# Windowed attention of a two-layer encoder: its loops taken apart into seven streams, TensorE's order written out

## The chip, the cores and the metric

One core of a Trainium2 chip runs the whole program. The metric is device time in microseconds (us), the median of repeated executions. TensorE is PE in the rows (its weight loads PEld), VectorE is DVE, ScalarE is ACT, GpSimd is POOL, SyncE is SP.

## The reference, cut to what matters

An encoder of two layers over 256 tokens of 1024 channels. Layer 0 mixes tokens by a recurrence (RWKV-7), layer 1 by attention; each layer is followed by a mixture of 32 experts (MoE), of which a token uses two. Each sub-layer is normalised, shifted, scaled and gated by six vectors ("modulations") computed from a conditioning vector. The change touches layer 1's attention alone:

```python
qkv = jnp.einsum('bsd,de->bse', h, w_qkv)            # 1024 -> 9216: 3 groups x (q,k,v) x 8 heads x 128
for gi, (window, dil) in enumerate(ATTN_GROUPS):     # (128,1), (512,4), (2048,16)
    o, lse = _dilated_group(q, k, v, slopes[gi], window, dil)   # softmax(q k / sqrt(128) - slope*|distance|) v
alpha = jax.nn.softmax(jnp.stack(lses), axis=0)      # the three groups weighed by their denominators
merged = jnp.sum(alpha[..., None] * o, axis=0)
return jnp.einsum('bsd,de->bse', merged, w_o)
```

## The kernel before, in words

Matmuls of the attention run on pairs of 16-bit numbers: `split` (L461) makes of a float32 tile a high half on ScalarE and the rest, a low half, on VectorE (or on GpSimd, L467, for the second half of two weight tiles in three), and `triple` (L1712) issues three matmuls: high by high, low by high, high by low.

**Projections.** `heads` (L1722) goes through four pairs of heads (hp), three groups (g) and q, k, v (j): 36 projections. Each takes one 1 MB weight tile off the ring `wring`, splits it in two halves (`weights`, L1703; two buffers of each kind, so that half n is split when half n-2 has been multiplied), and issues 8 steps of 6 matmuls of 256 columns into one of three PSUM banks (`pp`). The result is split again (`qh`, `ql`).

**Scores and values.** For a pair and a group, `scores` (L1788) multiplies q by k, adds the distance term and takes the maximum on VectorE (L1800, L1803), and takes exponentials with their sums on ScalarE (L1809). `merge` (L1812) makes of maxima and sums of the three groups the weights `wg`, in some fifteen VectorE operations on 4 elements a partition. `values` (L1831), for each of two heads, multiplies the exponentials by `wg` on VectorE (L1837), transposes them on TensorE (`eT`), splits them, multiplies them by v (`av`) and splits the result into `mh`, `ml`. The tiles of exponentials E exist once, so a pair's scores wait for the values of the pair before. Group 0's scores follow the projections of group 1; those of groups 1 and 2 follow the projections of group 2 (loop at L1873).

**Modulations.** 32 parts, each a 512 KB row block of `w_ada` off a ring of two (`aring`), are multiplied and added into `acc` on VectorE (L374, L376): four parts behind each of the first eight groups (L1881). After eight parts `ada` (L428) sums `acc` over the partitions on TensorE. For vectors 2 and 5 (the gates `ga`) this is one float32 product for each half of the columns, and each is added on VectorE (L448) to a bias that a DMA on ScalarE's queue brings (L442, held behind what ScalarE was given before it). There is one PSUM bank (`ada`) for all of this.

**Output.** `out_pairs` (L1693) scales the four weight tiles of the output projection by the gate on GpSimd (L590), splits and multiplies them (`wo`). Three of the four run while the last pair's values wait.

**Order.** A scheduler places each engine's instructions by priority (the order of the program text) as its own cost estimates let them become ready; a matmul of the attention may so be placed before or after its neighbours in the text. In layer 0, `weave` (L277) is used: generators (streams) yield, an account adds up TensorE's estimated time, `RANK` chooses among the streams that are ready, `OFFSET` shifts the priority of what a stream issues, and TensorE's instructions are pinned to that order (L263). All weight tiles (layer 0, MoE 0, qkv, output, MoE 1) come in one order through one ring on SP's queue, and a load starts when a buffer is free. The attention frees buffers for MoE 1's weights as it ends. What follows the attention is MoE 1 (`moe`, L1369) in eight quarters of 12 tiles, and the final norm.

Of the kernel before, what the change touches and what calls it, by code (L numbers as in the profile page):

```python
# [19 lines left out]
D = 1024  # L20
S = 256
# [213 lines left out]
def trunk(ctx, tc, names, aps, out, stages=("rwkv", "moe0", "attn", "moe1"), dbg=None, ring=2):  # L235
# [189 lines left out]

    ada_acc, modulations_attn = [], []

    def ada(i, m, k, tag="ps"):  # L428
# [9 lines left out]
        if k < KD - 1:  # L438
            return
        if m in (2, 5):  # L440
            g = gates[i, m] = const.tile([128, D], F32, name=f"ga{m}", tag=f"ga{m}", bufs=1)
            bias = nc.scalar.dma_start(out=g, in_=ap["p_adab"][i:i + 1, m * D:(m + 1) * D].to_broadcast([128, D]))  # L442
            tc.keep_in_program_order(bias)
            for c in range(2):
                s = slice(c * 512, c * 512 + 512)
                ps = bank(name="ada", tag=tag)
                mm(ps, ONES, acc[:, s])
                V.tensor_tensor(out=g[:, s], in0=g[:, s], in1=ps, op=ALU.add)  # L448
        else:
            ps = bank(name="ada", tag=tag)  # L450
            for n in range(8):
                mm(ps[:, n:n + 1], acc[:, n * 128:(n + 1) * 128], ONES[:, 0:1])
            ada_due.append((i, m, ps))
# [1268 lines left out]
    def heads(outer, mh, ml, before, c4):  # L1722
# [42 lines left out]
        QK = XSC * XSC  # L1765
        scale = 128 ** -0.5

        def project(hp, g):
            out = []
            for j in range(3):  # L1770
                with tc.issue_after(heads.hi[5].ins) if hp + g == 0 and j == 1 else nullcontext():
                    w = heads.w if hp + g + j == 0 else weights(
                        outer, stream.take(("qkv", hp, g, j)).rearrange("p (k n) -> p k n", k=KD),
                        pool_half=j != 1 and hp + g > 0)
                ps = bank(name="qkv", tag="pp")
                t = [(held, pool)[j // 2].tile([128, 2, S], F16, name=f"q{n}{g}{j}", bufs=1) for n in "hl"]
                for k in range(KD):
                    hk = (hh[:, k], hl[:, k])
                    lhs, rhs = (w[k], hk) if j < 2 else (hk, w[k])
# [4 lines left out]
                split(*(v.rearrange("p a n -> p (a n)") for v in t), ps, (scale if j == 0 else 1.0) / WSC)  # L1784
                out.append(t)
            return out

        def scores(hp, g, qkv, E, st):  # L1788

            q, k, _ = qkv  # L1790
            w = KW[g]
            for a in range(2):
                ps = bank(name="sc", tag="sc")
                for t in range(NTT):
# [6 lines left out]
                                       in1=ps[:, 0:NTT * w].rearrange("p (t n) -> p t n", t=NTT),  # L1801
                                       op0=ALU.mult, op1=ALU.add)
                V.tensor_reduce(out=st[:, :, a, 0], in_=e, axis=AX.X, op=ALU.max)  # L1803
            neg = pool.tile([128, NTT, 2], F32, name="neg", bufs=2)
            V.tensor_scalar(out=neg, in0=st[:, :, :, 0], scalar1=-1.0 / QK, scalar2=None, op0=ALU.mult)
            for a in range(2):
# [24 lines left out]
        def values(hp, a, qkv, E, wg):  # L1831

            eh, el = (pool.tile([128, 8, 128], F16, name=n) for n in ("eh", "el"))
            for g in range(3):
                for t in range(NTT):
                    e = E[g][:, a, t * KW[g]:(t + 1) * KW[g]]
                    V.tensor_scalar(out=e, in0=e, scalar1=wg[:, t, g, a:a + 1], scalar2=None, op0=ALU.mult)  # L1837
            blocks = [E[0][:, a, t * 256 + kt * 128:t * 256 + kt * 128 + 128] for kt in range(2) for t in range(NTT)]
            blocks += [E[g][:, a, t * 128:(t + 1) * 128] for g in (1, 2) for t in range(NTT)]
            for n in range(2):  # L1840
                ps = bank(name="eT", tag="eT")
                for b in range(4):
                    tr(ps[:, b * 128:(b + 1) * 128], blocks[4 * n + b])
                split(*(v[:, 4 * n:4 * n + 4].rearrange("p b n -> p (b n)") for v in (eh, el)), ps, WSC)
            po = bank(name="av", tag="eT")
            vcol = slice(a * 128, a * 128 + 128)

            def av(o, v, c, start, stop):
                triple(o, [t[:, v[1], vcol] for t in qkv[v[0]][2]],
                       [t[:, c].rearrange("p b n -> p (b n)") for t in (eh, el)], start, stop)  # L1850

            for kt in range(2):
# [5 lines left out]
            split(*(v[:, 2 * hp + a].rearrange("p (l r) -> p r l", r=NTT) for v in (mh, ml)),  # L1858
                  po[:, 0:S].rearrange("p (r l) -> p r l", r=NTT), 1.0 / WSC)

        c4.enter_context(banks(pp=3, sc=2, eT=2, ada=1))
        apool1 = modulations_of_attention()
        if "moe1" in stages:
            ext.extend(middle(1, 3))
        attn_shares = iter(ADA_ATTN)
        for hp in range(4):
            if hp == 3:
                modulations_attn[0].done()
                apool1.release()
                if "moe1" in stages:  # L1870
                    ext.extend(middle(1, 0))
            qkv, E, st = [], [], []
            for g in range(4):  # L1873
                if g < 3:
                    qkv.append(project(hp, g))
                for n in range(max(0, g - 1), g):
                    E.append(pool.tile([128, 2, NTT * KW[n]], F32, name=f"E{n}", bufs=1))
                    st.append(pool.tile([128, NTT, 2, 2], F32, name=f"st{n}", bufs=2))
                    scores(hp, n, qkv[n], E[n], st[n])
                if g < 3 and hp < 3:  # L1880
                    for a in itertools.islice(attn_shares, ADA_PARTS[3 * hp + g]):  # L1881
                        ada(*a, "ada")
            if hp == 3:
                held.release()
                if "moe1" in stages:
                    ext.extend(middle(1, 4))
            wg = merge(st)
            for a in range(2):
                values(hp, a, qkv, E, wg)
            if hp == 3:  # L1890
                po = {(t, c): bank(name="wo", tag="ada" if t + c == 2 else "pp")
                      for t in range(NTT) for c in range(2)}
                for _ in out_pairs(outer, range(3), po, mh, ml):
                    pass
        pool.release()
        return po

# [201 lines left out]
```

## Time and profile before

| | |
|---|---|
| time of three runs | 1194.68, 1184.44, 1194.64 us; median 1194.64 |
| profiled execution | 1175.46 us, span 1173.7 us |
| busy, share of the span | PE 88%, PEld 58%, DVE 53%, ACT 37%, POOL 13% |
| HBM read | 319.22 MB, 273 GB/s over the span |
| mean granted clock of TensorE | 0.951 of full |

The attention's first projection starts at 674 us and its last output product ends at 951 us. The rows further down are of these stretches; their times count from the span's start. A bracket at the end of a row of the timeline is the idle time of the engine before it and what ended it.

### The profile page before, as it was taken

Reading aid. Unit: us, or ns where it says so; the run is one execution under the profiler, and the core shown is the slowest. Engines: PE = TensorE matmul, PEld = TensorE weight load, DVE = VectorE, ACT = ScalarE, POOL = GpSimd, SP = SyncE. Lnnn points to the kernel's source line nnn. Section 1 sums busy time; section 2 is a strip of 40 time slices with the busy share of each in tenths; the row PEclk is TensorE's granted clock in tenths of the full one; section 3 lists DMA queues with packets and bytes.
Section 4 is the critical chain, followed back from the end, with each engine's and each line's share of the span. In section 5 each row is a group of like instructions: output and inputs, shape, how many; then the busy total and the mean of one; then the engine's idle time right before and its main releaser. Section 6 shows DMA issues by size and latency. Waiting matters only on the chain. (4 is left out here: it accounts for less than half of the span.)

```text
span 1173.7 us, 25024 instructions
## 1 busy us (share of the span) xinstructions
PE 1031.4 (88%) x10580; PEld 675.4 (58%) x10580; DVE 620.2 (53%) x1460; ACT 431.6 (37%) x913; POOL 149.7 (13%) x110
## 2 busy tenths in 40 slices
PE   7789889999988998978987899898979999789886
PEld 2666667766766555434442388687868754344422
DVE  4774678478585446212211367999984752121112
ACT  2544455455446342101000366656544621010012
POOL 1020010010012600000000012122472000000000
PEclk9789999899979999989998999999989999899999
DMA  9462524325243676998999987887745589999995
GB/s 366 179 237 77 181 77 151 109 95 168 74 131 129 269 288 251 388 418 358 421 420 421 420 358 266 310 303 275 282 145 171 209 339 409 413 370 421 420 422 234
DMA packets 53197, 322.01 MB, mean 274 GB/s; under 512 B 5922, under 2 KB 6562, under 8 KB 21458
## 3 DMA queue, kind: packets, MB, share of 16 engines
q1 hardware_dynamic: 51986, 315.88, 69.0%
q0 software_dynamic: 800, 3.36, 0.7%
q8 instruction: 87, 1.43, 0.5%
q10 hardware_dynamic: 288, 1.05, 0.3%
q14 instruction: 36, 0.29, 0.1%
HBM read 319.22 MB, written 1.05 MB: 273 GB/s over the span
## 5 line engine op out<-in xcount | busy, mean ns | idle before, releaser
L271 PE MATMUL gu<-wring,xT 128*32 128x512 f32 x1024 | 132.6, 616 | 16.8 <-PEq L1609 10.2
L376 DVE SCALAR_TENSOR_TENSOR acc<-aring,silu,acc 128x512 f32<-128x512 f32 x140 | 116.0, 860 | 17.5 <-DMA aring<-in_w_ada_dram 17.3
L467 POOL TENSOR_TENSOR wl<-wring,wh 128x1024 f16<-128x1024 f32 x24 | 57.0, 2377 | 403.4 <-ACT wh L466 400.9
L271 PE MATMUL qkv<-hh,wh 128*128 128x256 f16 x384 | 106.1, 276 | 1.8 <-ACT hh L1761 1.8
L271 PE MATMUL qkv<-hl,wh 128*128 128x256 f16 x384 | 105.7, 276 | 1.8 <-DVE hl L1762 1.8
L271 PE MATMUL qkv<-hh,wl 128*128 128x256 f16 x384 | 106.0, 276 | 1.2 <-DVE wl L473 1.2
L271 PEld LDWEIGHTS gu<-wring,xT 128*32 128x32 f32 x1024 | 30.8, 112 | 100.5 <-issue 82.0
L271 PEld LDWEIGHTS <-wh 128*128 128x128 f16 x768 | 76.1, 99 | 12.8 <-issue 3.5
L271 PE MATMUL dn<-wring,hidT 128*32 128x256 f32 x1024 | 65.5, 404 | 18.4 <-ACT hidT L1564 18.4
L473 DVE SCALAR_TENSOR_TENSOR wl<-wring,wh 128x1024 f16<-128x1024 f32 x56 | 70.5, 1264 | 16.4 <-ACT wh L469 16.3
L271 PE MATMUL acc<-y,back 128*128 128x512 f32 (+1 forms) x144 | 66.0, 581 | 10.3 <-DVE y L1591 8.1
L271 PEld LDWEIGHTS xT<-oh,x 128*128 128x128 f32 x512 | 59.0, 192 | 21.1 <-issue 9.2
L469 ACT ACTIVATE wh<-wring 128x1024 f16<-128x1024 f32 x56 | 58.6, 1050 | 33.0 <-PE qkv L271 23.2
L1366 DVE SCALAR_TENSOR_TENSOR sg<-sg,gu 128x256 f32<-128x256 f32 x16 | 6.7, 420 | 116.8 <-ACT sg L1365 116.8
L1591 DVE TENSOR_TENSOR y<-dn,ga 128x512 f32<-128x512 f32 x28 | 19.4, 692 | 88.3 <-PE dn L271 56.7
L271 PE MATMUL xT<-oh,x 128*128 128x128 f32 x512 | 63.5, 280 | 2.5 <-DVE oh L1475 2.5
L1365 ACT ACTIVATE sg<-gu 128x256 f32<-128x256 f32 x16 | 6.1, 384 | 145.6 <-PE gu L271 145.6
L271 PEld LDWEIGHTS dn<-wring,hidT 128*32 128x32 f32 x1024 | 31.9, 115 | 48.2 <-ACT hidT L1564 22.3
L1507 ACT ACTIVATE back<-bT 128x256 f32<-128x256 f32 x16 | 6.2, 386 | 131.0 <-PE acc L271 131.0
L271 PE MATMUL qkv<-wh,hh 128*128 128x256 f16 x192 | 52.3, 273 | 0.0
L271 PE MATMUL qkv<-wh,hl 128*128 128x256 f16 x192 | 52.3, 273 | 0.0
L271 PE MATMUL qkv<-wl,hh 128*128 128x256 f16 x192 | 52.3, 273 | 0.0
(355 smaller groups left out, 2090.4 us busy)
## 6 DMA issues: line engine op xcount, KB each, us to landing
wring<-in_w_moe_dram SPq DMA_DIRECT2D x192, 1024.0 KB, 19.8
aring<-in_w_ada_dram SPq DMA_DIRECT2D x96, 512.0 KB, 4.6
wring<-in_w_qkv_dram SPq DMA_DIRECT2D x36, 1024.0 KB, 8.4
wring<-in_w_kr_dram SPq DMA_DIRECT2D x8, 1024.0 KB, 5.9
wring<-in_w_vl_dram SPq DMA_DIRECT2D x8, 640.0 KB, 5.0
wring<-in_w_rwo_dram SPq DMA_DIRECT2D x4, 1024.0 KB, 8.1
wring<-in_w_ato_dram SPq DMA_DIRECT2D x4, 1024.0 KB, 6.6
x<-in_x_dram POOLq DMA_DIRECT2D x2, 512.0 KB, 7.2
```

The lines of the kernel that those rows point to most:

```text
L271: return on_pe(nc.tensor.matmul(out=o, lhsT=lhsT, rhs=rhs, start=start, stop=stop, **kw))
L376: V.scalar_tensor_tensor(out=acc[:, s], in0=w[:, s], scalar=silu[:, k:k + 1], in1=acc[:, s], op0=ALU.mult, op1=ALU.add)
L467: eng.tensor_tensor(out=lo, in0=src, in1=hi, op=ALU.subtract)
L469: A.activation(out=hi, in_=src, func=AF.Copy, scale=by)
L473: V.scalar_tensor_tensor(out=lo, in0=src, scalar=by, in1=hi, op0=ALU.mult, op1=ALU.subtract)
L1365: A.activation(out=o, in_=ps[:, 0:256], func=AF.Tanh, scale=0.5)
L1366: V.scalar_tensor_tensor(out=o, in0=o, scalar=1.0, in1=ps[:, 0:256], op0=ALU.add, op1=ALU.mult)
L1507: A.activation(out=back, in_=ps[:, 0:S], func=AF.Copy)
L1591: V.tensor_tensor(out=y, in0=py[c], in1=gates[i, 5][:, c * 512:(c + 1) * 512], op=ALU.mult)
```

## The change

The nested loop is replaced by seven generators that `weave` runs: K (weight tiles, one half at a time), P (splits of projections), T (scores), U (merge, weighing, values), N (modulations), Q (projections), O (output products). TensorE's instructions in the attention are now pinned to the order that the account gives. A stream yields a condition, or a number: the account's time until it counts as ready again (2.6 ahead of scores, 11.0 or 8.0 ahead of the transposes, 3.2 and 1.0 inside the values, 4.6 between parts of the modulations). Scores of a group become ready when its q and k are split, so ahead of its v projection. The multiplication by `wg` moves from VectorE to ScalarE. The modulation parts are no longer counted per group, and their sum over partitions is issued 4.6 after the eighth part. The output's first three weight tiles are split by half in stream K.

```diff
-RANK = dict(X=0, C=1, R=2, F=3, D=4, G=5, S=6, H=6, W=7, A=2.5)
-OFFSET = dict(X=0, C=-6, R=-4, F=-2, D=-2, G=-1, S=0, H=0, W=0, A=8)
-ADA_PARTS, PACE = (4, 4, 4, 4, 4, 4, 4, 4, 0), 4.0
+RANK = dict(X=0, ..., A=2.5, K=-1, P=-1, T=0, U=1, N=2, Q=8, O=9)
+OFFSET = dict(X=0, ..., A=8, K=0, P=-4, T=-4, U=-4, N=4, Q=0, O=0)
+PACE, ATTN_PACE = 4.0, 4.6
...
+        def all_weights():
...
+            for b in range(1, 36):
+                hp, g, j = b // 9, b // 3 % 3, b % 3
+                for k in range(2):
+                    yield after(("half", 2 * b + k - WB))
+                    if k == 0:
+                        w = stream.take(("qkv", hp, g, j)).rearrange("p (k n) -> p k n", k=KD)
...
+                        halves[2 * b + k] = half(w, KD, k, P if k and j != 1 and b >= 3 else None)
+                    done.add(("w", 2 * b + k))
+            for u in range(3):
+                for k in range(2):
+                    n = 72 + 2 * u + k
+                    yield after(("half", n - WB), ("modulations", 0))
+                    if k == 0:
+                        w = gated(stream.take(("ato", u)), gates[1, 2], 2).rearrange("p (k n) -> p k n", k=2)
...
+        def projections():
+            for b in range(36):
...
+                yield after(("split", b - 3))
                 ps = bank(name="qkv", tag="pp")
                 for k in range(KD):
+                    if k % 4 == 0:
+                        yield after(("w", 2 * b + k // 4))
...
+                    if k % 4 == 3:
+                        done.add(("half", 2 * b + k // 4))
+                    yield
...
+        def all_scores():
+            for hp in range(4):
+                for g in range(3):
+                    yield after(("split", 9 * hp + 3 * g + 1), ("values", hp - 1))
+                    yield 2.6
...
+        def all_values():
+            for hp in range(4):
+                yield after(("scores", 3 * hp + 2))
+                wg = merge([sts[hp, g] for g in range(3)])
+                E = [Es[hp, g] for g in range(3)]
+                for a in range(2):
+                    weigh(a, E, wg)
+                yield 11.0 if hp < 3 else 8.0
...
+        def attn_modulations():
+            for i, m, k in ADA_ATTN:
+                ada(i, m, k, "ada", False)
+                yield ATTN_PACE
+                if k == KD - 1:
+                    ada_total(i, m, ada_acc[-1], "ada")
...
+        def weigh(a, E, wg):
             for g in range(3):
                 for t in range(NTT):
                     e = E[g][:, a, t * KW[g]:(t + 1) * KW[g]]
-                    V.tensor_scalar(out=e, in0=e, scalar1=wg[:, t, g, a:a + 1], scalar2=None, op0=ALU.mult)
+                    A.activation(out=e, in_=e, func=AF.Copy, scale=wg[:, t, g, a:a + 1])
...
+        weave((all_weights(), "K"), (splits(), "P"), (all_scores(), "T"), (all_values(), "U"),
+              (attn_modulations(), "N"), (projections(), "Q"), (output(po), "O"))
```

`ada_total` is the part of `ada` from its test for the gates on: for a gate it issues the bias's DMA, then for each half of the columns the product and the addition, with no yield in between.

## Rows read from the trace of the kernel before

**Rows 1.** Chain of work that ended last: start us, us, what.
```profile
1061.43 7.00 PE gu L271 x62
1070.30 19.80 DMA wring<-in_w_moe_dram
1129.98 19.80 DMA wring<-in_w_moe_dram
```

**Rows 2.** Stretches: us, then PE, PEld, DVE, ACT, POOL busy, clock, DMA share, GB/s.
```profile
676.40:951.00 274.60, 254.43 (x2232) 211.94 (x2232) 219.29 (x371) 156.98 (x268) 77.48 (x38) 0.98 0.71 263
727.60:756.00 28.40, 24.21 (x218) 19.40 (x215) 28.14 (x63) 16.35 (x36) 4.40 (x3) 1.00 0.85 311
858.10:884.60 26.50, 18.09 (x166) 15.71 (x163) 23.12 (x47) 11.26 (x29) 18.39 (x11) 0.87 0.28 91
875.00:880.00 5.00, 5.00 (x39) 4.39 (x38) 4.15 (x13) 2.25 (x3) 0.84 (x1) 0.67 0.00 0
```

**Rows 3.** Waits of PE from 676.4 to 951: us in total, times, longest.
```profile
PE eT L275 <- DVE E L1837: 11.9, 4, 8.4
PE ada L271 <- DVE acc L376: 4.4, 4, 1.8
PE eT L275 <- DVE ml L473: 1.9, 1, 1.9
...
PE qkv L271 <- DVE wl L473: 1.2, 2, 0.7
```

**Rows 4.** Timeline of PE, 28 projection matmuls apart: start us, us, what.
```profile
861.19 0.27 PE L271 MATMUL qkv<-hh,wh 128*128 128x256 f16 x1
...
864.25 0.27 PE L271 MATMUL qkv<-hh,wl 128*128 128x256 f16 x1
```

**Rows 5.** Timeline of PE: last scores and first transpose, pairs 2 and 3.
```profile
859.06 0.22 PE L271 MATMUL sc<-ql,qh 128*128 128x128 f16 x1
...
874.68 0.48 PE L275 MATMUL eT<-cst,E 128*128 128x128 f32 x1 [8.41 <-DVE E L1837]
...
924.02 0.22 PE L271 MATMUL sc<-ql,qh 128*128 128x128 f16 x1
...
931.32 0.33 PE L275 MATMUL eT<-cst,E 128*128 128x128 f32 x1
```

**Rows 6.** Timeline of DVE (merges of pairs 2 and 3) and of POOL (gating).
```profile
865.05 2.35 DVE L1819 TENSOR_TENSOR wg<-st,mm 128x4 f32<-128x4 f32 x3
...
927.90 0.31 DVE L1819 TENSOR_TENSOR wg<-st,mm 128x4 f32<-128x4 f32 x3
...
861.37 11.95 POOL L590 TENSOR_TENSOR wring<-wring,ga 128x512 f32<-128x512 f32 x8
```

**Rows 7.** Weighing on DVE (timeline); exponentials on ACT (lines: busy us, mean ns).
```profile
874.28 1.92 DVE L1837 TENSOR_SCALAR E<-E,wg 128x256 f32<-128x256 f32 x8
...
L1809 ACT ACTIVATE E<-E,neg 128x128 f32<-128x128 f32 x32 | 12.4, 390 | 10.1 <-DVE neg L1805 10.1
...
L1809 ACT ACTIVATE E<-E,neg 128x256 f32<-128x256 f32 x16 | 7.9, 498 | 1.0 <-DVE neg L1805 1.0
```

**Rows 8.** Tile aring and line L442: ns min/median/max, first and last start; landings.
```profile
L376 DVE SCALAR_TENSOR_TENSOR acc<-aring,silu,acc x56: 735/747/2621, 703.1 to 839.3; 128x512 f32<-128x512 f32 x56
L153 SPq DMA_DIRECT2D aring<-in_w_ada_dram x32: 327/328/842, 680.4 to 833.8; - x32
...
DMA to landing us min/median/max: 3.4/4.6/10.6
...
DMA to landing us min/median/max: 3.7/3.7/3.7
```

**Rows 9.** Timeline of PE and DVE: the sum of gate 5, half by half.
```profile
839.44 1.12 PE L271 MATMUL ada<-acc,cst 128*128 128x512 f32 x2 [1.78 <-DVE acc L376]
...
850.07 0.68 DVE L448 TENSOR_TENSOR ga<-ga,ada 128x512 f32<-128x512 f32 x1
...
850.80 1.13 PE L271 MATMUL ada<-acc,cst 128*128 128x512 f32 x2 [0.19 <-DVE ga L448]
```

More of the change, by code (lines that the diff above doesn't have):

```diff
@@ L1766, in heads, with after @@
         scale = 128 ** -0.5
[L1768 to L1774, printed above, removed]
+        halves, done, qkvs, Es, sts = {}, set(), {}, {}, {}
+        def after(*what):
+            return lambda: all(w in done for w in what if w[1] >= 0)
@@ L1775, in project @@
+        def projections():
+            for b in range(36):
+                hp, g, j = b // 9, b // 3 % 3, b % 3
+                if b == 27:
+                    yield after(("modulations", 0))
+                    modulations_attn[0].done()
+                    apool1.release()
+                    if "moe1" in stages:
+                        ext.extend(middle(1, 0))
+                yield after(("split", b - 3))
                 ps = bank(name="qkv", tag="pp")
-                t = [(held, pool)[j // 2].tile([128, 2, S], F16, name=f"q{n}{g}{j}", bufs=1) for n in "hl"]
@@ L1783, in project @@
                                k == 0 and a == 0, k == KD - 1)
-                split(*(v.rearrange("p a n -> p (a n)") for v in t), ps, (scale if j == 0 else 1.0) / WSC)
-                out.append(t)
-            return out
+                    if k % 4 == 3:
+                        done.add(("half", 2 * b + k // 4))
+                    yield
+                qkvs[b] = ps
+                done.add(("project", b))
+            yield after(("scores", 11))
+            held.release()
+            if "moe1" in stages:
+                ext.extend(middle(1, 4))
@@ new lines, in splits @@
+        def splits():
+            for b in range(36):
+                hp, g, j = b // 9, b // 3 % 3, b % 3
+                yield after(("project", b), ("values", hp - 1) if j == 2 else ("scores", 3 * (hp - 1) + g))
+                t = [(held, pool)[j // 2].tile([128, 2, S], F16, name=f"q{n}{g}{j}", bufs=1) for n in "hl"]
+                split(*(v.rearrange("p a n -> p (a n)") for v in t), qkvs[b], (scale if j == 0 else 1.0) / WSC)
+                qkvs[b] = t
+                done.add(("split", b))
@@ new lines, in all_scores @@
+        def all_scores():
[3 more added lines that the diff above has]
+                    yield 2.6
+                    E = Es[hp, g] = pool.tile([128, 2, NTT * KW[g]], F32, name=f"E{g}", bufs=1)
+                    st = sts[hp, g] = pool.tile([128, NTT, 2, 2], F32, name=f"st{g}", bufs=2)
+                    yield from scores(hp, g, [qkvs[9 * hp + 3 * g + j] for j in range(2)], E, st)
+                    done.add(("scores", 3 * hp + g))
@@ new lines, in all_values @@
+        def all_values():
[6 more added lines that the diff above has]
+                yield 11.0 if hp < 3 else 8.0
+                yield after(*(("split", 9 * hp + 3 * g + 2) for g in range(3)))
+                for a in range(2):
+                    yield from values(hp, a, [qkvs[9 * hp + 3 * g + 2] for g in range(3)], E)
+                done.add(("values", hp))
@@ new lines, in attn_modulations, with output @@
+        def attn_modulations():
[4 more added lines that the diff above has]
+                    ada_total(i, m, ada_acc[-1], "ada")
+            ada_settle()
+            done.add(("modulations", 0))
+        def output(po):
+            yield after(("project", 35), ("split", 35))
+            for t in range(NTT):
+                for c in range(2):
+                    po[t, c] = bank(name="wo", tag="ada" if t + c == 2 else "pp")
+            for k in range(6):
+                yield after(("w", 72 + k))
+                for t, c in po:
+                    triple(po[t, c], (mh[:, k, t * 128:(t + 1) * 128], ml[:, k, t * 128:(t + 1) * 128]),
+                           [v[:, c * 512:(c + 1) * 512] for v in halves[72 + k][0]], k == 0, False)
+                    yield
+                done.add(("half", 72 + k))
@@ L1788, in scores @@
         def scores(hp, g, qkv, E, st):
[L1790 removed]
+            q, k = qkv
             w = KW[g]
@@ L1864, in heads @@
             ext.extend(middle(1, 3))
[L1865 to L1894, printed above, removed]
+        po = {}
+        weave((all_weights(), "K"), (splits(), "P"), (all_scores(), "T"), (all_values(), "U"),
+              (attn_modulations(), "N"), (projections(), "Q"), (output(po), "O"))
         pool.release()
```

31 lines of the change are left out of this document (24 added, 7 removed).

## The prediction

> **What bounds the kernel now.** I read the chain that ended last first, then the stretches, then TensorE's waits inside the attention. The chain ends in a run of MoE weight loads from 1070 to 1150, each released by the one before; ahead of it stands TensorE's own work [rows 1]. So the last 100 us follow the transfers, but these were let go by buffers that TensorE freed, and those began with the attention's end. Over the whole stretch after the attention the DMA engines were 92% busy, inside it 71% [rows 2]. An attention that ends X earlier frees every later buffer X earlier, while the transfers keep 29% of the attention's time to spare; I therefore count a gain or loss in the attention one for one at the end.
>
> Inside the attention TensorE is the bound: busy 254.4 of 274.6 us, against 219.3 for VectorE, 157.0 for ScalarE and 77.5 for GpSimd [rows 2]. The work itself stays: 36 projections of 48 matmuls at 0.109 each (28 of them in 3.06 [rows 4]) are 189 us, and scores, transposes, values and output keep their number. What the change can move is the 20.2 us of idle time, and the clock. The waits say where it lies: 11.9 + 1.9 on the transposes, which wait for weighed exponentials or the split before; 4.4 where modulations are summed; 1.2 on low halves of weights [rows 3], together 19.4. The wait of 8.4 ahead of pair 2's transposes [rows 5] is followed by 5 us at a mean granted clock of 0.67, between the levels of 1.2 and 2.4 GHz [rows 2], while TensorE was busy: 0.33 x 5 = 1.7 lost. **At most 21.1 us can be won**, 1.8% of the span.
>
> **The change part by part.**
>
> *Scores at once, pinned order.* One step of a projection is 6 x 0.109 = 0.66 us of real time, and 6 x 256/2400 + 0.12 = 0.76 in the account. The 11.0 between scores and transposes are thus 15 steps, 9.8 us; the 2.6 are 4 steps, 2.6 us; 8.0 before the last pair's are 11 steps of output work or projections, some 7.2 us. What does the chain from the last score to the first transpose need? For pair 3 it took 931.32 - 924.24 = 7.1, for pair 2 it took 874.68 - 859.28 = 15.4 [rows 5]. The new chain is shorter, since group 1's four exponentials per pair are done long before: 4 x (0.39 + an accumulator read that I leave out) = 1.6 less [rows 7]; and longer by ScalarE's weighing of the first two tiles, 2 x (0.498 - 0.24) = 0.5 [rows 7]. So 6.0 where nothing is in the way and 14.3 where VectorE is as loaded as in pair 2, against 9.8 granted. Since TensorE's order is pinned, what is missing becomes idle time. For pairs 0 and 1 I take 1.5 each, nearer the short end, because weighing leaves VectorE, which was busy 28.1 of 28.4 us behind pair 0 [rows 2]; bounds 0 and 4.5. For pair 2 the gating of the output weights on GpSimd is not moved by the change: it starts when a ring buffer frees, so it still covers the merge. Three subtractions on 4 elements took 2.35 us while GpSimd was gating, 0.31 in pair 3 without it [rows 6]. I take 3.5 for pair 2, near the long end (4.5), and no clock loss, the waits of 1.9 and 1.8 having left none that I could see. Pair 3: 6.0 against 7.2, nothing. Scores wait for a split that has 2.6 us and shares its engines with weights: 12 times 0.1, 1.2 in all; bounds 0 and 0.5 each, 6.0.
>
> *Weighing on ScalarE.* 16 + 32 instructions leave VectorE (6 per head at 0.24 undisturbed [rows 7], 11.5 us in all) and come to ScalarE at the cost of an exponential of their size (16 x 0.498 + 32 x 0.390 = 20.4, an estimate from [rows 7]; the operations differ, bounds 15 and 25). ScalarE goes from 57% to 65% of the stretch, VectorE from 80% to 76%. This lies beside TensorE's work except at the head of the chain, priced above. Its cover is the granted 9.8 us; behind it on ScalarE stand the high halves of the next weights, for which TensorE would wait if the six instructions went in one row of 2.6.
>
> *Modulations.* The 32 parts stay: their DMAs, their place behind weight tiles on SP's queue, and 2 x 0.747 on VectorE each [rows 8]. They now stand 4.6 apart from the start, and TensorE meets the first sum 36.7 us after its projections run, near 676.5 + 2 + 36.7 = 715. The first two loads were issued at 680.4 and one took 10.6 [rows 8], so adding can't begin much before 691; with two buffers a part takes (4.6 + 1.5)/2 = 3.05 at best, eight end at 715.4. That is just in time, with nothing to spare. Then the halves of a gate: one bank, no yield between them, so the second product waits in TensorE's fixed order for the addition (0.68), and that for the bias, which lands 3.7 after its issue [rows 8]. Before, TensorE put 10 us of projections between the two halves of gate 5 [rows 9]; this cover is gone. For each gate 0.7 to 5 us; I take 3 for the first, where the parts are late too, and 2 for the other. The two sums into columns: 0.9 each, as before (4.4 over four [rows 3]); bounds 0 and 1.8.
>
> *Output, weight halves.* The same splits two halves ahead, the same three tiles behind the last projection; TensorE has output work to do while pair 3 waits, as now. Nothing, and no DMA is added.
>
> **The sum.** Removed 21.1. New: 3.0 + 3.5 + 1.2 + 5.0 + 1.8 = 14.5. Gain 6.6 us. The profiled execution took 1175.46 (span 1173.7 and 1.8 around it) and would take 1168.9; the median of the runs shown is 1194.64, 1.6% above it, and they spread over 10 us. On the median's scale the gain is 6.6 x 1.016 = 6.7: **1187.9 us**. With all new waits at their low ends (1.4) the gain is 19.7, 1174.6; at their high ends (9.0 + 4.5 + 6.0 + 10.0 + 3.6 = 33.1) it is a loss of 12.0, 1206.8.
>
> **Rivals.**
>
> *Packed.* The granted times suffice and TensorE runs without a wait but for the gates' additions (about 3): gain 18, **1176.3**. For it: VectorE is busy only 80% of the stretch, and bursts, four parts of modulations behind each group, are what filled it to 99% behind pair 0 [rows 2]; even pacing takes them away. Against it: the gating on GpSimd, and the bias.
>
> *Late sums in a fixed order (slower).* Place: the four sums. Parts of the modulations have the latest priority (+4) on a VectorE that is still over 90% busy while they last; if each sum finds its eighth part 5 us late, TensorE idles 20, and twice 4.4 for the bias and the addition, with 7.7 for the rest and 2 for a lower clock: 38.5 new against 21.1, a loss of 17.4 x 1.016: **1212**. It turns slower when sums and gates cost more than 13.4 together. For it: eight parts end just when TensorE comes, and the second half of gate 5 waited on the bias until 850 [rows 9]. Against it: the 4.6 ahead of each sum, and waits on sums were 1.8 at most [rows 3].
>
> *Weighing on the slower engine.* Six weighings take 4 x 0.390 + 2 x 0.498 = 2.6 on ScalarE and 1.4 on VectorE [rows 7]; if the transposes of all 8 heads waited for the difference of 1.1, 9 us go and a loss of 2.4 stays: **1197**. Against it: 9.8 us are granted and the second head's weighing lies behind the first head's values. The Trainium skill, "ScalarE: Activation LUTs", section "Rules for kernel authors", says the same thing as a rule: multiplications belong on VectorE, not on ScalarE. By that rule this part alone is a loss; the rows agree on the durations, and what they show beside it is that VectorE was the engine TensorE waited for.
>
> *It doesn't reach the end.* Transfers, not buffers, set the end, and a shorter attention only makes them queue: **1194.6**. Against it: the idle 29%.
>
> **How the numbers follow.** Forecast (some waits go, others come) 0.50, packed 0.23, late sums 0.15, slower weighing 0.08, not reaching the end 0.04. About 1% (12 us) is what a measurement of this kernel can tell from no change. Faster by more: most of packed (0.21) and the better quarter of the forecast's spread (0.14), 0.35. Slower by more: most of late sums (0.13) and 0.02 of the forecast, 0.15. The rest, 0.50, within 1%. The range goes from 1173, packed with the runs' spread, to 1203, the forecast's bad end with gates and scores high; it leaves out late sums.
>
> **What would show it.** In the profile after: waits of the transposes on weighed exponentials down from 11.9 to about 6, now on ScalarE's weighing, and the longest not 8.4 but under 6, at pair 2. Waits ahead of the sums up, the second product of a gate waiting for the addition of the first (it waited 0.19 [rows 9]), 1 to 5 us. VectorE below 100% behind pairs 0 and 1. The attention's stretch at some 268 us, and the rest of the span unchanged, the same chain of transfers at its end, 7 us earlier. The forecast is wrong if gates wait 5 or more each, if pair 2's merge runs free of the gating, or if the transfers after the attention show new idle time.

## The result, and the profile after

The changed kernel is slower. Its median is 1216.21 us over 4 executions (1209.57 to 1221.14), the kernel before's, measured beside it, 1193.18 over 4 (1184.44 to 1194.68); the recorded ratio is **1.0241, interval 1.02 to 1.0282**, 28.8 us on that median. The two medians alone differ by 23.0, a ratio of 1.0193, so the size is less sure than the interval says; the direction is not in doubt, since no execution of the one lies among the other's. The prediction was 1187.9 with a range of 1173 to 1203, and the time lies outside it. What came is the rival that had 0.15, "late sums in a fixed order", priced at 1212.

The profiled execution of after took 1221.14 us, that of before 1175.46: 45.7 more. Part of that gap lies between executions: after's attention starts 6.1 us later (682.5 against 676.4) behind instructions that the change doesn't touch. The attention itself takes 310.50 us against the 274.60 of [rows 2], 35.9 more, and from its end to the span's end another 3.6 are added.

Stretches of the trace after (us, then PE, PEld, DVE, ACT, POOL busy, granted clock, DMA share, GB/s): the whole attention, the hole at the first gate and the 5 us behind it, the time around the last gate, and in it the 6 us behind that gate's hole.

```profile
682.50:993.00 310.50, 261.62 (x2234) 215.66 (x2234) 209.78 (x322) 170.20 (x317) 73.66 (x38) 0.93 0.65 236
...
724.00:744.00 20.00, 0.00 (x0) 0.00 (x0) 10.04 (x14) 5.29 (x6) 0.00 (x0) 0.63 0.74 275
744.00:749.00 5.00, 3.88 (x4) 1.15 (x5) 1.64 (x3) 1.06 (x1) 0.00 (x0) 0.50 1.00 419
863.80:896.80 33.00, 21.75 (x163) 16.68 (x161) 14.38 (x21) 13.29 (x27) 11.27 (x7) 0.84 0.36 131
...
880.00:886.00 6.00, 5.59 (x20) 3.33 (x21) 1.04 (x2) 0.00 (x0) 4.36 (x4) 0.50 0.00 0
```

The 35.9 us have two parts. TensorE is idle 310.50 - 261.62 = 48.9 us instead of 20.2: 28.7 more. And it is busy 7.2 us longer with the same matmuls, because behind each hole it ran at the lower level for a while: 0.50 of full speed, 1.2 GHz, at 744 to 749 and at 880 to 886, where the stretch behind the old hole had a mean of 0.67 [rows 2]. VectorE was busy only half of the 20 us in which TensorE did nothing at all, so this was not VectorE at its limit either.

Waits of PE in the attention of after (us in total, times, longest):

```profile
PE ada L271 <- DVE acc L376: 20.3, 1, 20.3
PE qkv L271 <- DVE wl L476: 12.8, 8, 4.4
PE ada L271 <- DVE ga L451: 9.6, 2, 8.8
PE qkv L271 <- ACT wh L472: 2.1, 3, 1.0
...
PE sc L271 <- DVE ql L476: 1.4, 3, 0.5
```

Beside [rows 3]: the waits of 11.9 and 1.9 on the transposes have no row any more; one wait at a sum's accumulator, four times 4.4 in all before, is now 20.3 at once; the addition of a gate's halves, 0.2 before, is 9.6; the low halves of weights, 1.2 before, are 12.8.

Timeline of PE after (start us, us, engine, line, tiles, idle before and releaser): the last projection matmul ahead of the first gate, both halves of its sum; those of the last gate; and the two places where pair 2 could have waited.

```profile
723.73 0.27 PE L271 MATMUL qkv<-hl,wh 128*128 128x256 f16 x1
744.35 2.08 PE L271 MATMUL ada<-acc,cst 128*128 128x512 f32 x2 [20.35 <-DVE acc L376]
747.20 2.07 PE L271 MATMUL ada<-acc,cst 128*128 128x512 f32 x2 [0.78 <-DVE ga L451]
...
870.58 1.02 PE L271 MATMUL ada<-acc,cst 128*128 128x512 f32 x2
880.41 2.08 PE L271 MATMUL ada<-acc,cst 128*128 128x512 f32 x2 [8.80 <-DVE ga L451]
...
912.77 0.28 PE L271 MATMUL qkv<-hh,wl 128*128 128x256 f16 x1 [4.42 <-DVE wl L476]
...
915.61 1.06 PE L275 MATMUL eT<-cst,E 128*128 128x128 f32 x4
```

The projections that follow the gate in the order, from 749.07 to 760, took no wait; the sum ahead of them did. With its order fixed, TensorE stood still for 20.35 us and then took 2.08 for a product that takes 1.02 at the full clock (870.58; the granted clock just ahead of it is 1.00).

Was the sum later than before? Timeline of PE in the kernel before, the first gate's sum (the first of its two matmuls; it took no wait):

```profile
736.76 0.70 PE L271 MATMUL ada<-acc,cst 128*128 128x512 f32 x1
```

That is 60.4 us behind the attention's start; in after the sum runs at 744.35, 61.9 behind it. So VectorE had the eight parts together about when it had them before. What changed is the place of the sum in TensorE's order: 41.5 us behind the start (724.0), some 19 ahead of that. Why it could not be ready at 41.5 stands in VectorE's rows.

Timeline of DVE after, columns as above: the parts of the first gate and the additions of the gates' halves; the merge of pair 2.

```profile
726.38 1.23 DVE L476 SCALAR_TENSOR_TENSOR wl<-wring,wh 128x1024 f16<-128x1024 f32 x1 [0.67 <-ACT wh L472]
727.52 2.73 DVE L376 SCALAR_TENSOR_TENSOR acc<-aring,silu,acc 128x512 f32<-128x512 f32 x4
732.53 1.42 DVE L376 SCALAR_TENSOR_TENSOR acc<-aring,silu,acc 128x512 f32<-128x512 f32 x2 [2.28 <-DMA aring<-in_w_ada_dram]
736.29 1.41 DVE L376 SCALAR_TENSOR_TENSOR acc<-aring,silu,acc 128x512 f32<-128x512 f32 x2 [2.34 <-DMA aring<-in_w_ada_dram]
738.13 1.42 DVE L376 SCALAR_TENSOR_TENSOR acc<-aring,silu,acc 128x512 f32<-128x512 f32 x2 [0.42 <-DMA aring<-in_w_ada_dram]
743.54 1.41 DVE L376 SCALAR_TENSOR_TENSOR acc<-aring,silu,acc 128x512 f32<-128x512 f32 x2 [3.99 <-DMA aring<-in_w_ada_dram]
...
879.66 0.69 DVE L451 TENSOR_TENSOR ga<-ga,ada 128x512 f32<-128x512 f32 x1 [6.41 <-DMA ga<-in_p_adab_dram]
...
902.31 3.21 DVE L1923 TENSOR_TENSOR wg<-st,mm 128x4 f32<-128x4 f32 x3
```

Parts 3 and 4 are taken together at 727.52 with no wait for a transfer: they lay in the buffers (asked for at 709.50 and 711.42, and no part took over 11.0 to land), and VectorE's own order had them behind the weights' halves. Only then did the two buffers come free, and parts 5 to 8 each waited for their own transfer (2.28, 2.34, 0.42, 3.99). The last part was added by 744.95, and TensorE had been there since 724.0. At the last gate the sum was in time, but its bias was not: VectorE waited 6.41 us for that transfer and TensorE 8.80 for VectorE. ScalarE's queue issued it at 873.30, 2.7 behind the start of the sum's first product, and it took 6.3 to land.

Tile aring after (durations ns min/median/max, first and last start us), and its transfers:

```profile
L153 SPq DMA_DIRECT2D aring<-in_w_ada_dram x32: 327/328/384, 686.4 to 854.6; - x32
L374 DVE TENSOR_SCALAR acc<-aring,silu x8: 480/481/486, 708.6 to 832.8; 128x512 f32<-128x512 f32 x8
...
DMA to landing us min/median/max: 3.4/5.6/11.0
```

The first part was asked for at 686.4 and no part took over 11.0 to land, so it was there by 697.4; VectorE took it at 708.6.

The chain that ended last, after (start us, us, what), against [rows 1]:

```profile
1101.42 1.93 PE acc L271 x4
1103.34 19.79 DMA wring<-in_w_moe_dram
...
1143.07 19.87 DMA wring<-in_w_moe_dram
...
1162.99 1.98 PE gu L271 x8
```

It has the same form: TensorE's work, then weight loads back to back, now three from 1103.34 instead of four from 1070.30. A longer attention arrives at the end whole.

### The profile page after: what moved, and what is told of

It is laid out like the page before. It is cut to its first block, busy times and chain, and to the rows that moved or that the text cites. A ratio compares the mean times of both kernels' runs of the same rounds, so it can differ in the third digit from the quotient of the medians.

```text
span 1219.3 us, 25048 instructions
## 1 busy us (share of the span) xinstructions
PE 1046.5 (86%) x10580; PEld 682.3 (56%) x10580; DVE 609.9 (50%) x1412; ACT 444.6 (36%) x961; POOL 146.0 (12%) x110
## 5 line engine op out<-in xcount | busy, mean ns | idle before, releaser
L376 DVE SCALAR_TENSOR_TENSOR acc<-aring,silu,acc 128x512 f32<-128x512 f32 x140 | 113.4, 837 | 27.6 <-DMA aring<-in_w_ada_dram 27.5
L271 PE MATMUL dn<-wring,hidT 128*32 128x256 f32 x1024 | 67.2, 412 | 18.1 <-ACT hidT L1567 18.1
L271 PEld LDWEIGHTS xT<-oh,x 128*128 128x128 f32 x512 | 59.0, 192 | 21.1 <-PE gu L271 9.2
L1594 DVE TENSOR_TENSOR y<-dn,ga 128x512 f32<-128x512 f32 x28 | 19.4, 692 | 90.0 <-PE dn L271 60.8
```

What stands on the lines that cost most here:

```text
L271: return on_pe(nc.tensor.matmul(out=o, lhsT=lhsT, rhs=rhs, start=start, stop=stop, **kw))
L376: V.scalar_tensor_tensor(out=acc[:, s], in0=w[:, s], scalar=silu[:, k:k + 1], in1=acc[:, s], op0=ALU.mult, op1=ALU.add)
L1594: V.tensor_tensor(out=y, in0=py[c], in1=gates[i, 5][:, c * 512:(c + 1) * 512], op=ALU.mult)
```

## The experiments

All ratios are to the kernel before, measured beside each. "Attention" is the stretch as in [rows 2], from 2.4 us behind the first projection matmul to the last output matmul, in the profiled execution (for sums_free in the one of sums_free_look).

| kernel | ratio | 95% | attention us |
|---|---|---|---|
| after | 1.0241 | 1.02 to 1.0282 | 310.5 |
| weigh_dve | 1.0312 | 1.0255 to 1.0368 | 322.9 |
| bias_early | 1.0189 | 1.0142 to 1.0236 | 300.1 |
| sums_later | 1.0127 | 1.0078 to 1.0176 | 298.9 |
| sums_apart | 1.0078 | 1.0046 to 1.0111 | 289.6 |
| apart_ring3 | 1.0024 | 0.9997 to 1.0051 | 284.1 |
| sums_free | 0.9976 | 0.9945 to 1.0007 | 280.4 |
| unpinned_bias | 0.9975 | 0.9941 to 1.0008 | 277.6 |
| unpinned | 0.9962 | 0.9934 to 0.999 | 275.2 |
| before_weigh_act | 0.9949 | 0.9915 to 0.9984 | 277.3 |
| before_act_ring3 | 0.9938 | 0.9912 to 0.9964 | 274.2 |

The theory: TensorE's order puts the gates' sums where the account has them ready, the parts and the bias come later than that, and the fixed order turns the difference into idle time with a slow restart. The rivals: the fixed order costs whatever it is that comes late (weights' halves, splits); ScalarE's weighing costs it.

**unpinned**: the streams, the early scores and ScalarE's weighing stay, TensorE's order in the attention is left to the scheduler.

```
-    def weave(*streams):
+    def weave(*streams, pin=True):
-        base, now, pinned[0] = tc.cur_priority, 0.0, True
+        base, now, pinned[0] = tc.cur_priority, 0.0, pin
...
-              (attn_modulations(), "N"), (projections(), "Q"), (output(po), "O"))
+              (attn_modulations(), "N"), (projections(), "Q"), (output(po), "O"), pin=False)
```

> The changed kernel with TensorE's instructions in the attention not pinned to the account's order (streams, early scores and ScalarE's weighing stay). Late sums in a fixed order (after waits 20.3 + 9.6 us at the sums, and works slowly behind them): the waits at the sums fall to 5 us or less, ratio to the kernel before 0.99 to 1.005. ScalarE's weighing, or scores crowding VectorE: the waits on weights' halves (14.9 us) stay and the ratio stays above 1.015.

Measured 0.9962. Waits of PE in its attention (us in total, times, longest):

```profile
PE eT L275 <- ACT E L1939: 4.4, 3, 2.6
PE qkv L271 <- DVE wl L476: 3.6, 3, 2.6
PE ada L271 <- DVE ga L451: 3.4, 1, 3.4
...
PE ada L271 <- DVE acc L376: 1.5, 2, 1.1
```

The same work with a free order has no wait over 3.4 us, so the whole loss of after hangs on the fixed order: 1.0241 against 0.9962, 2.8% or 33 us. The first sum ran 64.0 us behind the attention's start, with a wait of 0.35 ahead of it: TensorE had other work until then. It does not yet say on what in the order the loss hangs.

**sums_later**: the modulations' stream starts 22 us later in the account, sums and additions alike.

```
         def attn_modulations():
+            yield 22.0
             for i, m, k in ADA_ATTN:
```

> The changed kernel with the first part of the modulations ready 22 later in the account, so that TensorE meets the first sum some 19 us later; all else, the pinned order too, as in the change. Late sums: the wait of 20.3 us at the first sum falls under 3 and the slow clock behind it goes, 20 to 25 us less than after, ratio 1.000 to 1.008; the wait of 8.8 us inside the last gate's sum stays. If the fixed order as such costs the time, the wait only moves to other places and the ratio stays at 1.02.

Measured 1.0127, outside the range expected: half of the loss goes. The wait at the first accumulator fell to 10.7, not under 3: TensorE came to the sum 15.9 us later than in after (57.4 behind the start), but VectorE's additions slid with the stream too (the sum ran 68.1 behind the start, in after 61.9). The last gate, which was late for its bias, still cost 11.6.

**bias_early**: each gate's bias is asked for at the gate's first part instead of at its sum.

```
         ada_add(acc, w, k, k == 0)
+        if k == 0 and not whole and m in (2, 5):
+            ada_bias(i, m)
```

> The changed kernel with a gate's bias loaded when the first of its eight parts is added, in place of right ahead of its sum. Late sums: the wait of 8.8 us between the two halves of the last gate falls under 2.5, with some 2 us of slow clock, ratio 1.013 to 1.018; the first sum's wait of 20.3 us stays, since its parts are late and not its bias. If the bias is not what the addition waits for, nothing changes: 1.024.

Measured 1.0189, just outside the range expected (1.013 to 1.018). Waits of PE (us in total, times, longest; the lines have moved by six):

```profile
PE ada L271 <- DVE acc L376: 19.4, 1, 19.4
PE qkv L271 <- DVE wl L482: 12.2, 7, 3.5
PE ada L271 <- DVE ga L457: 3.1, 2, 2.3
```

The wait at ga fell from 9.6 to 3.1, the others stayed. The intervals of this ratio and after's overlap, so its size in time is not settled; its place is.

**weigh_dve**: the changed kernel with the weighing back on VectorE (`V.tensor_scalar(out=e, in0=e, scalar1=wg[:, t, g, a:a + 1], ...)` for the activation with that scale).

> The changed kernel with the weighing back on VectorE. Late sums: within 0.4% of after, 1.020 to 1.028, since no wait of the transposes is left to shorten and 12 us of work come back to VectorE. ScalarE's weighing as the cause: waits on the halves of weights fall from 14.9 to under 7 and the ratio to 1.015 or less.

Measured 1.0312, above the 1.020 to 1.028 expected. The waits at acc (21.8) and wl (14.8) grew, that at ga (9.1) stayed. ScalarE's weighing is not what made the change slow.

**sums_free**: the order stays fixed for all of TensorE's work in the attention but the sums; the rest is chained past them.

```
     def on_pe(i):
-        return tc.keep_in_program_order(i) if pinned[0] else i
+        if loose[0]:
+            apart_.add(i.ins.name)
+        elif pinned[0]:
+            prev = next(p for p in reversed(nc.cur_bb.bb.instructions)
+                        if p is not i.ins and p.engine == i.ins.engine and p.name not in apart_)
+            tc.add_manual_dep(i.ins, prev.name, ...)
+        return i
...
+                    loose[0] = True
                     ada_total(i, m, ada_acc[-1], "ada")
+                    loose[0] = False
```

> The changed kernel with TensorE's order still fixed by the account for everything in the attention except the sums of the gates and columns (ada_total): these ten matmuls of 512 and sixteen columns-groups are left for the scheduler to place, and the rest is chained past them. Theory 'late sums in a fixed order': the waits acc (20.3 us), ga (9.6 us) and the slow clock behind them go, the rest of the fixed order stays, so the attention goes from 310 to about 277 to 283 us and the ratio to the kernel before to about 0.995 to 1.005; the waits for the weights' halves (wl 12.8, wh 2.1) may stay. Rival 'the fixed order as a whole' (any late operand costs, the sums are only the first): the waits move to wl, wh, ql and eh, the attention stays over 295 us and the ratio over 1.012.

Measured 0.9976, as the theory had it. Its profiled execution ran TensorE at half rate throughout (last section) and is not in the ratio; for its waits the kernel was run once more.

**sums_free_look**: the same kernel.

> The same kernel as sums_free once more, for its trace (in the profiled execution of sums_free TensorE ran at half rate throughout, 534 ns for a 128x256 matmul of the projections, so its waits can't be read). Theory 'late sums in a fixed order': acc and ga together under 6 us of TensorE's waits, wl and wh under 7 (they were a consequence of twelve additions of parts in a row on VectorE), attention 275 to 283 us. Rival 'the fixed order as a whole': wl, wh, ql, el and E together over 15 us, attention over 290 us.

The attention took 280.4 us. Waits of PE (lines moved by seven):

```profile
PE qkv L278 <- DVE wl L483: 11.3, 6, 3.5
PE ada L278 <- DVE ga L458: 2.4, 1, 2.4
...
PE ada L278 <- DVE acc L383: 1.7, 1, 1.7
```

acc and ga are 4.1 together, as expected; **wl is 11.3 where I had expected under 7**: the waits for weights' halves were not a consequence of the late sums. With the halves made by GpSimd (0.8) and ScalarE (0.5) they come to 12.6, against 5.9 in unpinned (3.6 and 2.3). In time they weigh little, sums_free and unpinned being within each other's intervals. So 2.65 of the 2.8% go with the sums' fixed places; what is left is 0.1%, which these runs don't tell from nothing.

**sums_apart**: everything is fixed; the account sets the first gate's sum 20 us behind its last addition, and the bias is early.

```
                 yield ATTN_PACE
                 if k == KD - 1:
+                    if m == 2:
+                        yield 20.0
                     ada_total(i, m, ada_acc[-1], "ada")
```

> The changed kernel with the whole order fixed as before, but the account puts the sum of the first gate 20 us behind the part's last addition (only there), and asks for each gate's bias at the gate's first part. The loads of the parts keep their times in the account. Theory 'the account places the sums ahead of VectorE's additions': the wait of 20.3 us at acc falls to under 5, that of 8.8 at ga to under 2, the granted clock behind the first gate stays near 1, the attention takes 275 to 287 us and the ratio is 0.995 to 1.01. Rival 'VectorE's order is made from TensorE's, so the additions slide with the sum' (as when the whole stream was delayed by 22 us and the wait only halved): the wait at acc stays over 8 us, the attention stays over 293 us, ratio over 1.012.

Measured 1.0078, in the theory's range; the waits and the attention (289.6, expected 275 to 287) missed it. Waits of PE:

```profile
PE ada L271 <- DVE acc L376: 10.4, 3, 5.9
PE ada L271 <- DVE ga L457: 7.4, 2, 6.6
```

The waits at acc are 10.4 in all and 5.9 at the first gate, not under 5: TensorE came to the first sum 18.1 us later than in after, and VectorE's additions slid by 3.7. The waits on weights' halves are 5.9 in all (4.3, 0.8 and 0.8), in a fully fixed order, as few as in unpinned: the 12.6 of sums_free_look don't come from the fixed order alone.

**apart_ring3**: sums_apart with three buffers in the parts' ring (`bufs=2` and the stream's depth 2 to 3).

> sums_apart with three buffers instead of two in the ring of the parts (aring). In sums_apart each of the parts 5 to 8 of the first gate waited for its own landing, 3.6 to 5.2 us behind the issue that the freed buffer allowed, and the sum still waited 5.9 us at acc. If the round trip of the ring of two sets that: the wait at acc falls to under 2.5 us and the ratio from 1.0078 to 1.001 to 1.005. If VectorE's own order sets it (its additions sit behind the merge and the halves of the weights): acc stays at 5 to 8 us and the ratio at 1.006 to 1.01.

Measured 1.0024, the number that the round trip was to give. Waits of PE:

```profile
PE ada L271 <- DVE ga L457: 11.3, 2, 8.8
PE qkv L271 <- DVE wl L482: 7.0, 5, 3.5
...
PE ada L271 <- DVE acc L376: 0.7, 1, 0.7
```

The number came, the mechanism only in part. In sums_apart none of VectorE's idle time around the first gate is put down to a part's transfer, so the expectation started from a wait that isn't there. Against sums_apart VectorE had the first sum's parts 2.1 us earlier behind the attention's start, and TensorE came 4.1 later, in part for a longer wait on a low half of weights (3.5 against 1.7); together that takes the 5.9 away. The waits at ga and wl grew by 3.9 and 2.7, and the intervals of the two ratios overlap. A fully fixed order is thus not told from before (1.0024, 0.9997 to 1.0051), but unpinned (0.9934 to 0.999) is faster. What is left at ga is not the bias now. Timeline of DVE, around the last gate (first half of the sum done by 868.8):

```profile
868.86 2.34 DVE L1931 TENSOR_TENSOR wg<-st,mm 128x4 f32<-128x4 f32 x3
...
876.24 0.69 DVE L1937 TENSOR_TENSOR den<-den,mm 128x4 f32<-128x4 f32 x1
876.86 0.67 DVE L457 TENSOR_TENSOR ga<-ga,ada 128x512 f32<-128x512 f32 x1
```

VectorE's order has pair 2's merge ahead of the addition, and that merge is slow under GpSimd's gating, 2.34 us where it takes 0.31 alone [rows 6].

**before_weigh_act**: the kernel before with ScalarE's weighing alone.

> The kernel before with one part of the change alone: the 48 multiplications of the exponentials by their weights go from VectorE (0.31 and 0.2 us each) to ScalarE (0.39 and 0.5 us each). Theory: VectorE is what TensorE's transposes wait for behind the merge (E 11.9 us in all), ScalarE has idle time there, and the scheduler can still put other work in front; a gain of 0 to 6 us, ratio 0.995 to 1.00. Rival by the Trainium skill's page 'ScalarE: Activation LUTs' (section 'Rules for kernel authors'), plain multiplications being cheaper on VectorE: each merge to transposes path is longer by 2 to 4 us, 6 to 12 us in all, ratio 1.005 to 1.01.

Measured 0.9949, the theory's lower edge: a small gain by itself. The transposes' wait on weighed exponentials is 8.7 in 2 pieces, 11.9 in 4 before [rows 3]; the attention of the profiled execution doesn't show the gain (277.3 against 274.6).

**unpinned_bias**: unpinned and bias_early together.

> The changed kernel without the fixed order in the attention (ratio 0.996 before) and with each gate's bias asked for at the gate's first part, so that its landing can't be late. If the 3.4 us that TensorE waited at ga there came from the bias: 3 to 4 us less, ratio 0.992 to 0.995. If from VectorE's addition of the halves: no change, ratio 0.995 to 0.998.

No change to unpinned: 0.9975, wait at ga 2.8 for 3.4. With a free order the bias wasn't what the addition waited for.

**before_act_ring3**: the kernel before, ScalarE weighing, three buffers in the ring.

> The kernel before with ScalarE weighing (0.9949 alone) and three buffers in the ring of the parts. TensorE's waits at acc there are 4.5 us in 3 pieces; without a fixed order the scheduler already puts other work before the sums, so 0 to 3 us less: ratio 0.992 to 0.996. If the third buffer's earlier loads delay the weights of the projections behind them in the DMA engines: 0 to 3 us more, 0.995 to 0.998.

Measured 0.9938, interval 0.9912 to 0.9964, median 1177.9: faster than before and than after. Waits of PE in its attention:

```profile
PE eT L275 <- ACT E L1837: 8.7, 2, 6.8
PE qkv L271 <- DVE wl L473: 4.2, 3, 1.8
...
PE ada L271 <- DVE acc L376: 2.3, 4, 0.9
```

acc fell from 4.4 [rows 3] to 2.3, and the third buffer delayed nothing that shows in the time. The interval overlaps that of before_weigh_act (0.9915 to 0.9984), so a gain of the buffer isn't shown.

## Why the prediction was wrong

**The bound, and "one for one at the end": right.** The attention grew by 35.9 us in the trace, the stretch from its start to the span's end by 39.5 (1219.3 - 682.5 against 1173.7 - 676.4); the 3.6 beyond one for one are not explained. The 92% that the argument used stands in no row of [rows 2]; the stretch 951 to 1173.7 has it (DMA share 0.92). The 21.1 to be won took the waits listed, 19.4; with all the idle time of 20.2 it is 21.9.

**Scores at once, transposes: right in direction, the places changed.** The 13.8 us of the transposes' waits are gone, more than forecast. Pairs 0 and 1 took none of the 3.0 that I put there. For pair 2 the merge did stay under the gating (902.31, 3.21 us against 2.35 in [rows 6]), as forecast; but TensorE's wait of 4.42 came at a projection three us ahead of the transposes, for a low half of weights that VectorE had behind the merge. The 3.5 I had for it were of the right size and one tile off. The scores' splits cost 1.4 + 0.7, forecast 1.2.

**Weighing: right as a cost, and a small gain by itself.** The lines of after show what ScalarE paid (busy us, mean ns of one):

```profile
L1939 ACT ACTIVATE E<-E,wg 128x128 f32<-128x128 f32 x32 | 10.1, 386 | 0.0
...
L1939 ACT ACTIVATE E<-E,wg 128x256 f32<-128x256 f32 x16 | 7.2, 494 | 6.3 <-DVE wg L1932 6.3
```

386 and 494 against the 390 and 498 that I took from the exponentials. One by one they are dearer than on VectorE, and the Trainium skill, "ScalarE: Activation LUTs", section "Rules for kernel authors", would have them on VectorE. The measurement decides against it here: on the kernel before the part alone is 0.9949 (0.9915 to 0.9984), and taken back out of after it is 1.0312 for 1.0241 (the intervals overlap). I read it so that VectorE is the engine on which TensorE's operands are late, and ScalarE has time; no run separates this reading from others.

**Modulations: the step that failed.** "That is just in time, with nothing to spare": I had TensorE at the first sum 38.7 us behind the attention's start, and it came 41.5 behind it (724.0), so that half held. The eighth part I had at 715.4, on after's start 721.4; it was added by 744.95, 23.5 later. The term was worked out from the transfers: a part could be added as soon as it had landed, at 691, and then one each 3.05 us. VectorE didn't do that. It took the first part at 708.6, 11.6 later than the 697.0 that this means on after's start; the third at 727.52, 18.9 behind the first where two periods of 3.05 are 6.1, 12.8 more; from there to the end it needed 17.4 us for six parts, where I had 18.3, 0.9 less. So against my sum the loss lies in when VectorE reached the first and the third part; the round trips behind them (9.0 us of waits for transfers from 727.52 on) were in the sum already. The third part's transfer was asked for at 709.50, so it lay there by 720.5 at the latest, 7.0 before VectorE took it. What in VectorE's order put it there no run shows: with a third buffer (apart_ring3) the third part was added at 709.12 and the fourth only at 728.10, so the gap stays with the first part that needs a freed buffer. **Rows that I had said it**: in [rows 8] the additions of the kernel before at L376, those of the second part on, begin at 703.1, 26.7 behind the attention's start; in after they begin at 710.0, 27.5 behind it. Had I begun there instead of at a landing, the eighth part would have ended at 703.1 + 7 x 3.05 = 724.5, some 9 us behind the sum's place: new waits of about 23.6 against 21.1, a small loss, still inside the range. The row that gives the rival's price is the sum itself: in the kernel before it ran 60.4 behind the start (736.76), where I put it at 38.7, so 21.7 ahead: 14.5 + 21.7 = 36.2 of new waits, a loss of 15.1, some 1210 (an estimate). Taking "the engine adds when the data is there" for an engine that is 80% busy and has its own order was the error.

**The gates' halves: mis-sized.** Forecast 3 and 2; measured 20.35 + 0.78 and 8.80. For the last gate the 0.7 to 5 had the bias landing 3.7 after an issue at the sum; it was issued 2.7 behind the first product's start and took 6.3 to land. With the bias early the wait was 2.3 (bias_early, the addition ahead of the merge), 6.6 and 8.8 (sums_apart and apart_ring3, the merge ahead of it). [rows 9] I had misread: in the kernel before, gate 5's bias was issued at 844.56 and landed 3.7 later, by 848.3; the addition began at 850.07 directly behind a low half of weights, so VectorE's order and not the bias set the 850. The columns' sums cost nothing, where I had 1.8.

**Weights' halves: forecast nothing, measured 14.9** (12.8 + 2.1). With all halves counted they are 12.6 in sums_free_look and 5.9 in unpinned, but also 5.9 in sums_apart, where everything is fixed. So they are no cost of the fixed order as such; what makes them is open, and they weigh little in time.

**The clock: forecast no loss.** TensorE's busy time grew by 7.2 us. I judged from waits of 1.9 and 1.8 us; the waits of 20.35 and 8.80 are another case, and both levels stand in the rows: 2.08 us for a product behind each, 1.02 ahead of the second.

**The rival** was right in its place, its sign and nearly its price (1212 against 1216.21), with another make-up: not four sums 5 us late each, but one 20 and one 9, and a slower clock of 7 where it had 2. That its price came so near is in part luck. I gave it 0.15 on the row that waits on sums were 1.8 at most. That row came from a kernel in which the scheduler put other work ahead of a late sum; it could say nothing on how late sums are once that is not allowed.

**Open.** No run gave the parts another place in VectorE's order, and the third buffer was not tried on after alone. The early scores were not run alone. Why sums_free's waits on weights' halves (11.3) hardly show in its time was not pursued. The profiled execution of before is 1.5% under its median, so its 274.6 us may be a short attention: unpinned has 275.2 and is faster.

## What to carry to other kernels

Before an engine's order is fixed, list for each instruction that gets a place whose engine's queue its operand comes out of, and read from the trace when that engine did the work before, or when the instruction itself ran (here 60.4 us behind the start, where the new order put it at 41.5), not when it could have; what has the last priority there (sums, gates, biases) should stay free or get its place from that row. A small wait for an operand in a freely ordered kernel is no bound on its lateness, since other work was put ahead of it. If a fixed order is wanted all the same, the place of the late instruction is what to move: 20 us more in the account, with the bias early, took the ratio from 1.0241 to 1.0078. One more buffer behind it took the wait at the sums from 10.4 to 0.7 us, but other waits grew, and its gain in time is not clear of the noise.

## What the hardware showed

In one execution of sums_free TensorE ran at half rate from beginning to end, 2469 us, with a granted clock recorded as 1.00 all along. Line of the page of that execution (busy us, mean ns of one):

```profile
L278 PE MATMUL qkv<-hh,wh 128*128 128x256 f16 x384 | 205.1, 534 | 1.6 <-ACT hh L1771 1.6
```

In after the same matmul has a mean of 280 ns, slow stretches included. The other ten executions took 1176.6 to 1190.8 us. A granted clock of 1.00 is thus no proof of full speed; the duration of a known matmul showed it. Nothing here says what caused it.

Three subtractions of 4 elements took VectorE 3.21 us, against 0.31 without GpSimd at work [rows 6]. Timeline of POOL after, beside them (they began at 902.31):

```profile
897.48 5.93 POOL L593 TENSOR_TENSOR wring<-wring,ga 128x512 f32<-128x512 f32 x4
903.38 2.12 POOL L470 TENSOR_TENSOR wl<-wring,wh 128x1024 f16<-128x1024 f32 x1
```

One of the three took 1.12 and ended at 903.43, as the gating ended (903.41); one took 2.09 and ended at 905.52, as GpSimd's split of a weight ended (905.50); the third took 0.15. So not the gating alone makes the merge slow. The Trainium skill, "SBUF — State Buffer", section "SBUF: two separate sides", has an exclusive lock between these two engines, for a VectorE instruction with two operands in SBUF against a GpSimd instruction that reads SBUF, under which one waits out the other's instruction whole; the rows agree with that in size and in where the two ends fall, and no run here separates it from another cause.
